# A gated three-branch decoder layer: two gates computed ahead of the stick-breaking branch, which is gated as it leaves PSUM, and the weight sums issued at other rates

## The chip, the core and the metric

The kernel runs on one core of a Trainium2 chip. Its engines are TensorE (PE, matrix products, whose results go to banks of the PSUM memory), VectorE (DVE) and ScalarE (ACT), which work on tiles of 128 partitions in SBUF or PSUM, GpSimd (POOL) and SyncE (SP), which here mostly issue DMA transfers. The metric is device time in microseconds, as the median of several runs; a single profiled execution gives the trace from which durations are read.

## The reference

One layer (batch 1, 512 tokens, model width 1024) with three causal token mixers: A differential attention (4 heads), B stick-breaking attention (8 heads), C dilated windows (4 heads in each of 3 groups). Each branch is projected to the model width, gated, and the three are summed:

```python
proj = x @ w_in          # q, k, v of the three mixers, and three gates of 1024 columns
o_da = diff_attention(...); o_sb = stick_breaking_attention(...); o_dl = dilated_attention(...)
g = jax.nn.sigmoid(gates).reshape(B, S, N_BRANCHES, D)
merged = (g[:, :, 0] * (o_da @ w_branch_da) + g[:, :, 1] * (o_sb @ w_branch_sb)
          + g[:, :, 2] * (o_dl @ w_branch_dil))
m = merged @ w_out
x = layer_norm(alpha * x + m, ln1_g, ln1_b)
c = jnp.square(jax.nn.relu(x @ w_up)) @ w_down
ple = jax.nn.sigmoid(x @ w_ple_gate) * (p @ w_ple)
x = layer_norm(alpha * x + c + ple, ln2_g, ln2_b)
```

Everything is float32.

## The kernel before

**Products.** A float32 product is made of three matmuls in a rounded format: each operand is split into a high part (a cast on ACT, L264) and the rest (a subtraction on DVE, L266), and high x high, high x low and low x high are summed in PSUM. Weights come in chunks of 128 x 1024 (512 KB): SP loads a chunk into one of 6 raw buffers (`fill`, L196), the two splits write one of 5 pairs of tiles (`split_next`, L240), and the matmuls read those. All other tiles of 128 x 512 come from one pool of 52 slots (`slot`, L76): a tile gets a slot when the last reader of the one before is done, be it an engine or a DMA.

**Seven products for eight.** Many of the large products are cut in 2 x 2 x 2 blocks and made with seven block products in place of eight (`seven`, L720, for gates; `value_pair`, L545; `group_items`, L355; and others). Four of the seven need sums of weight blocks. Most sums are made ahead in DRAM by DMAs that POOL issues, some of which add while they write (`sum_steps`, L1197): 15 targets or pairs of targets for the mixers, then those of the MLP, four at a time in turn. Others (products 7 and 3 of the value pair and the gates) are made by a DMA that adds onto a raw chunk once that chunk has been split (`then_add`, L173).

**The list of items.** The program is a list of items. An item is a burst of matmuls into a PSUM bank and an eviction, which is emitted after the next item's weights have been split. In order, with the item's number: the q, k and v projections of B (0 to 10), q and k of the dilated heads 0 and 1 and the values of group 0 (11 to 26), the values of A (27 to 30), the values of groups 1 and 2 as a "value pair" (31 to 44, 12 matmuls each), q and k of the dilated heads 2 and 3 in three groups of 7 items (45 to 58 and 63 to 69, 24 matmuls of 256 columns in each item), q and k of A (59 to 62 and 70 to 73). Then the branch of B (`first_branch`, L816, 8 items of 12 matmuls, 74 to 81), the gate of B (`gate_alone`, L758, 14 items of 12, 82 to 95), the gate and branch of C (`gate_chain`, L787, and `branch_seven`, L876, 14 items of 12 and 14 of 6, 96 to 123), the gate and branch of A (124 to 151), the output projection, the first LayerNorm, the gated embedding and the MLP.

**Gates.** `gate_alone` frees each PSUM bank at once: its evictions are copies and additions into SBUF. `gate_chain` keeps up to six banks over several products and evicts less. Both leave raw gates in `gate_raw`. `gate_sig` (L685) makes one sigmoid on ACT, and only after the last exponential of the heads. The branch of B leaves PSUM as a copy on ACT (L832) into a new slot; its gating is a multiplication on DVE in SBUF (`first_gate`, L943), spread over the eight items after `gated_at`.

**Heads.** The attention heads are generators beside the items: `step` (L2122) advances each active head by one part, once or twice per item, and starts new heads as PSUM banks allow. A dilated head (`dil_head`, L1962) makes its scores and weights, waits for the values, takes some further empty steps (L2057), transposes the weights and makes its second product (L2087 and L2092) with `values`, which `keep` (L533) stored to DRAM and `values_of` (L537) loads again in strided order. Both are DMAs that POOL issues. All heads must be done at `gated_at - 1`; what is left of them is emitted there at once. The outputs of the heads of B and C are stored to DRAM (`put_away`) and loaded again by SP (`bring_back`) 9 items ahead of their branch for B, 14 for C.

**Pacing.** After each item the loop adds size x rate to a credit and issues one step of the weight sums for each whole unit (L2203 to L2209). A sum's DMA also waits for a split (or an eviction) four marks back, so that sums are spread over the main stream. From `forms_at` (item 25) up to `gated_at`, weight splits are ordered behind the latest ACT and DVE work of the heads (`tied`, L2189).

Of the kernel before, what the change touches and what calls it, by code (L numbers as in the profile page):

```python
# [57 lines left out]
def trunk(tc, a, out):  # L58
    nc = tc.nc
    es = ExitStack()  # L60
    with es:
# [14 lines left out]
        def slot(name, dt=F32):  # L76
            return big.tile([P, 512], dt, name=nm(name), tag="s", bufs=NSLOT)
# [146 lines left out]
        tied = [False]  # L224
# [61 lines left out]
        items = []  # L286
# [68 lines left out]
        def group_items(gi, pairs):  # L355
# [21 lines left out]
            def add(ps, need, free, run, ev, bank):  # L377
                for p in ps:
                    at = {5: 0, 6: 1, 7: 2, 3: 3}.get(p)
                    cs[p] = [chunk(w[{1: 0, 2: 1, 4: 3}[p]] if at is None else qsum[gi][at], 1024)]  # L380
                item([c for p in free for c in cs[p]], lambda b: run(), lambda b: ev(),
                     need=[c for p in need for c in cs[p]], bank=bank)
                items[-1]["rate"] = 0.85

            def put(*args):
                with tc.high_priority():
# [158 lines left out]
        def value_pair(nv):  # L545


            pair_at.append(len(items))
            cs, s, x = {}, {}, {}
            w = [[a["wv"][nv + n, 2 * h + kp].rearrange("p k n -> p (k n)") for n in range(2) for h in range(2)]  # L550
                 for kp in range(2)]

            for p in (1, 2, 7, 6, 4, 5, 3):
                for r in range(2):
                    if not r:
                        cs[p] = [chained(cs, p, kp, w[kp], vsum[kp]) for kp in range(2)]

                    def bank(p=p, r=r):
                        if p == 5:
                            x[r] = at_bank()  # L560
                        return x[r] if p in (5, 3) else at_bank() if r else mm_bank()

                    def mm(ps, p=p, r=r):
                        for k in range(4):
                            c = cs[p][k // 2]
                            n = slice(k % 2 * 512, k % 2 * 512 + 512)
                            q = slice(r * P, r * P + P)
                            h, lo = [t[:, q] for t in xf[p][k]]
                            go, end = k == 0 and p != 3, k == 3 and p != 5
                            nc.tensor.matmul(ps, h, c["h"][:, n], start=go, stop=False, skip_group_check=True)  # L570
                            nc.tensor.matmul(ps, h, c["l"][:, n], start=False, stop=False, skip_group_check=True)
                            nc.tensor.matmul(ps, lo, c["h"][:, n], start=False, stop=end, skip_group_check=True)

                    def ev(ps, p=p, r=r):
                        if p in (1, 7):
                            s[p, r] = slot("dl_v")
                            nc.scalar.copy(s[p, r], ps)
                        elif p == 2:
                            t = slot("dl_v")
                            nc.vector.tensor_add(t, s[1, r], ps)  # L580
                            keep(1, r, t)
                        elif p == 6:
                            nc.vector.tensor_add(s[1, r], s[1, r], ps)
                            nc.vector.tensor_add(s[7, r], s[7, r], s[1, r])
                        elif p == 3:
                            nc.vector.tensor_add(s[1, r], s[1, r], ps)
                            keep(1, 2 + r, s[1, r])
                        else:
                            t = slot("dl_v") if p == 4 else s[7, r]
                            nc.vector.scalar_tensor_tensor(t, s[7, r], -1.0, ps, op0=OP.mult, op1=OP.subtract)  # L590
                            keep(2, r + 2 * (p == 5), t)
                    item(cs[p] if r else [], mm, ev, need=cs[p], bank=bank, size=0.5)
                    items[-1]["rate"] = 1.0

        def v_items(nv, name, g):
            cs = [chunk(a["wv"][nv, c].rearrange("p k n -> p (k n)"), 1024) for c in range(4)]
# [29 lines left out]
            for tt in range(4):  # L626
                def mm(ps, tt=tt):
                    if name != "sb_v" or tt > 1:
                        products(ps, tt, range(4))
                        yield  # L630
                        products(ps, tt, range(4, 8))
                        return
                    if not tt:
                        two[0], two[1] = ps, mm_bank()
                    products(two[0], 0, range(4 * tt, 4 * tt + 4))
                    if tt:
                        put(two[0], 0)
                    yield
                    products(two[1], 1, range(4 * tt, 4 * tt + 4))

                def ev(ps, tt=tt):
                    if name != "sb_v" or tt:
                        put(two[1] if name == "sb_v" and tt == 1 else ps, tt)
                first = name == "sb_v" and tt < 2
                item(cs if tt == 3 else [], mm, ev, need=cs[2 * tt:2 * tt + 2] if first else cs,
                     bank=((lambda: two[0]) if tt else at_bank) if first else None)
                items[-1]["rate"] = 1.0 if name == "da_v" else 2.4

        nt, nv = 2, 0
        pair_at = []  # L650
# [29 lines left out]
        merged = {}  # L680
# [4 lines left out]
        def gate_sig(i, tt, half):  # L685
            t, sign = gate_raw.pop((i, tt, half))

            with tc.issue_after(last_exp[0]):
                nc.scalar.activation(t, t, AF.Sigmoid, scale=sign)
            return t  # L690
# [125 lines left out]
        def first_branch():  # L816
            for half in range(2):
                cs = [chunk(a["wb"][half, c].rearrange("p k n -> p (k n)"), 1024) for c in range(2)]
                for tt in range(4):
                    def mm(ps, tt=tt, cs=cs):  # L820
                        q = slice(tt * P, tt * P + P)
                        for k in range(4):
                            c = cs[k // 2]
                            n = slice(k % 2 * 512, k % 2 * 512 + 512)
                            h, lo = oTs[4 + k]
                            nc.tensor.matmul(ps, h[:, q], c["h"][:, n], start=k == 0, stop=False)
                            nc.tensor.matmul(ps, h[:, q], c["l"][:, n], start=False, stop=False)
                            nc.tensor.matmul(ps, lo[:, q], c["h"][:, n], start=False, stop=k == 3)

                    def ev(ps, tt=tt, half=half):  # L830
                        t = slot("b1")
                        e = nc.scalar.copy(t, ps)  # L832
                        marks.append(getattr(e, "ins", e))
                        merged[tt, half] = t
                    item(cs if tt == 3 else [], mm, ev, need=cs, size=0.5,
                         bank=at_bank if tt == 1 and not half else None)
                    items[-1]["rate"] = 2.4

        bsum = {i: [dram.tile([P, 1024], F32, name=f"bsum{i}_{j}") for j in range(4)] for i in (0, 2)}
        of = {}  # L840
# [97 lines left out]
            item([], mm, ev, size=0.08)  # L938

        for j, it in enumerate(items):  # L940
            it.setdefault("rate", 3.0 if j < 12 else 2.8 if j < 24 else 0.0 if j < 27 else 2.1)

        def first_gate(tt, half):  # L943
            g = gate_sig(1, tt, half)
            nc.vector.tensor_mul(merged[tt, half], merged[tt, half], g)

        branch_at = {1: len(items)}
        first_branch()
        gate_alone(0, 1)
        gated_at = len(items)  # L950
        for n, i in ((1, 2), (2, 0)):
            gate_chain(n, i)
            if n == 1:
                for j, th in enumerate([(tt, half) for half in range(2) for tt in range(4)]):
                    items[gated_at + 2 + j]["pre"] = lambda th=th: first_gate(*th)
            branch_at[i] = len(items)
            branch_seven(i, {} if i else {(6, 0): [(0, 0, 0)], (6, 1): [(0, 0, 1)], (5, 1): [(1, 0, 0)],
                                          (3, 0): [(1, 0, 1)]})
# [1003 lines left out]
        def dil_head(hd):  # L1962
# [91 lines left out]
            if hd == 0:  # L2054
                yield
                values = values_of(hd)
            for _ in range({0: 4, 1: 1, 3: 1}.get(hd, 0)):  # L2057
                yield

            src0 = {}  # L2060
# [4 lines left out]
            for half in range(2):  # L2065
# [4 lines left out]
                t = slot("pt0")  # L2070
# [4 lines left out]
            for g in range(2):  # L2075
# [4 lines left out]
                t = slot("pt12")  # L2080
# [4 lines left out]
            for kb in range(4):  # L2085
                n = 256 if kb < 3 else P
# [71 lines left out]
        for n, it in enumerate(items):  # L2158
# [27 lines left out]
            pump(freed, {1: 3, 3: 0, 4: 0, ple_at: 0, ple_at + 1: 0}.get(n, 1 if n < 10 else 2))  # L2186
            if n == 8:
                tie.clear()
            tied[0] = forms_at <= n < gated_at  # L2189
            if n == gated_at:  # L2190
                tie.clear()
            if n == 4:
# [165 lines left out]
```

## Time and profile before

| | |
|---|---|
| median of 3 runs | 1044.06 us (1042.19, 1044.06 and 1699.26) |
| profiled execution | 1043.86 us, its span 1042.2 us |
| mean granted clock of TensorE | 0.994 |
| VectorE, ScalarE, GpSimd busy | 778.8, 613.1, 203.7 us |
| moved by DMA | 270.74 MB, mean 260 GB/s |
| first branch and gate of B in the trace | matmuls at L826 to L828 from 418.8 us, at L735 to L737 from 453.3 us |

The span runs from the first to the last instruction of the trace; the time of the execution is 1.7 us longer. In the profile, a row names line, engine, operation and the tiles written and read (out<-in); `wh` and `wl` are the high and low part of a weight chunk, `graw` a raw gate, `b` a branch, `dl_vh` the reloaded values, `at` and `mm` PSUM banks. Matmuls are pipelined, so the duration of one is longer than the distance to the next. The granted clock is 1 where TensorE runs at full speed.

### The profile page before, as it was taken

How to read it: one execution, taken by the hardware profiler on the slowest of the kernel's cores; microseconds unless marked ns; L12 is line 12 of the kernel's file. 1: busy time of each engine (PE TensorE's matmuls, PEld its weight loads, DVE VectorE, ACT ScalarE, POOL GpSimd, SP SyncE). 2: the span in 40 equal slices, each digit the busy share in tenths (PEclk: the TensorE clock that was granted, in tenths of full speed). 3: DMA queues.
4: the chain of work that ended last, by engine and by line, in shares of the span. 5: the costliest groups of instructions: out<-in, count | busy, mean ns of one | idle time of the engine just before them, and what ended most of it. 6: DMA issues, size and time to landing. Idle time of an engine off the chain costs nothing.

```text
span 1042.2 us, 15650 instructions
## 1 busy us (share of the span) xinstructions
PE 1024.0 (98%) x5650; PEld 885.6 (85%) x5650; DVE 778.8 (75%) x1387; ACT 613.1 (59%) x1057; POOL 203.7 (20%) x307
## 2 busy tenths in 40 slices
PE   9999999999989999999999999999999999999997
PEld 7888888887979898878888888889999899899886
DVE  6888566758646877668879795898778777777975
ACT  7565556655534566555775753676666556566651
POOL 0323331112243012211112131211111121101001
PEclk9999999999989999999999999999999999999999
DMA  8999998659999789688999996489999999988522
GB/s 307 295 276 293 247 300 269 172 141 271 319 324 319 248 261 283 144 222 204 288 289 256 291 344 210 107 215 362 318 304 339 311 323 345 295 270 286 179 83 81
DMA packets 79534, 270.74 MB, mean 260 GB/s; under 512 B 9721, under 2 KB 12553, under 8 KB 79457
## 3 DMA queue, kind: packets, MB, share of 16 engines
q0 software_dynamic: 36624, 130.89, 50.1%
q1 hardware_dynamic: 42256, 137.95, 36.1%
q8 instruction: 44, 0.72, 0.3%
q10 hardware_dynamic: 576, 0.92, 0.2%
q14 instruction: 34, 0.27, 0.1%
HBM read 262.35 MB, written 112.22 MB: 359 GB/s over the span
## 4 chain that ended last, share of the span: by engine, by line
PE 74%; DMA 10%; DVE 6%; issue 6%; ACT 2%; POOL 1%; DVEq 0%; POOLq 0%; ACTq 0%
PE mm L89 6%; PE mm L90 6%; PE mm L91 6%; PE at L1415 4%; PE at L1416 4%; PE at L1417 4%; PE at L735 3%; PE at L736 3%; PE at L737 3%; DMA qsum<-qsum 2%; DMA msum<-in_wgm_dram 2%; DMA values<-dl_v 2%; DVE wl L266 2%; PE at L91 1%; PE at L90 1%
## 5 line engine op out<-in xcount | busy, mean ns | idle before, releaser
L266 DVE TENSOR_TENSOR wl<-raw,wh 128x1024 fp32r<-128x1024 f32 x268 | 322.1, 1214 | 118.3 <-ACT wh L264 115.4
L264 ACT CAST wh<-raw 128x1024 fp32r<-128x1024 f32 x268 | 276.2, 1042 | 197.5 <-PE mm L90 94.7
L89 PE MATMUL mm<-xhT,wh 128*128 128x512 f32 (+1 forms) x254 | 95.7, 377 | 0.0
L91 PE MATMUL mm<-xhT,wl 128*128 128x512 f32 (+1 forms) x254 | 94.3, 371 | 0.0
L90 PE MATMUL mm<-xlT,wh 128*128 128x512 f32 (+1 forms) x254 | 94.1, 371 | 0.0
L1415 PE MATMUL at<-wh,hh 128*128 128x512 f32 x188 | 73.7, 392 | 0.0
L1416 PE MATMUL at<-wl,hh 128*128 128x512 f32 x188 | 73.7, 392 | 0.0
L89 PE MATMUL mm<-x1hT,wh 128*128 128x256 f32 x256 | 72.8, 284 | 0.7 <-ACT up L1343 0.7
L1417 PE MATMUL at<-wh,hl 128*128 128x512 f32 x188 | 73.1, 389 | 0.0
L90 PE MATMUL mm<-x1lT,wh 128*128 128x256 f32 x256 | 72.4, 283 | 0.0
L91 PE MATMUL mm<-x1hT,wl 128*128 128x256 f32 x256 | 72.4, 283 | 0.0
L91 PEld LDWEIGHTS mm<-xhT,wl 128*128 128x128 f32 x254 | 47.8, 188 | 8.3
L89 PEld LDWEIGHTS mm<-xhT,wh 128*128 128x128 f32 x254 | 47.9, 188 | 7.8 <-PE mm L604 0.2
L90 PEld LDWEIGHTS mm<-xlT,wh 128*128 128x128 f32 x254 | 48.0, 189 | 7.5
L89 PEld LDWEIGHTS mm<-x1hT,wh 128*128 128x128 f32 x256 | 48.9, 191 | 2.7 <-ACT up L1343 0.9
L90 PEld LDWEIGHTS mm<-x1lT,wh 128*128 128x128 f32 x256 | 48.9, 191 | 1.5
L91 PEld LDWEIGHTS mm<-x1hT,wl 128*128 128x128 f32 x256 | 48.9, 191 | 0.0
L1232 POOL DMA_DIRECT2D usum<-in_wu_dram x32 | 28.5, 899 | 99.6 <-DVE wl L266 38.4
L1232 POOL DMA_DIRECT2D dsum<-in_wd_dram x28 | 23.4, 835 | 116.5 <-DVE wl L266 48.3
L1417 PEld LDWEIGHTS at<-wh,hl 128*128 128x128 f32 x188 | 35.3, 188 | 7.7
L1415 PEld LDWEIGHTS at<-wh,hh 128*128 128x128 f32 x188 | 35.5, 189 | 6.1
L1416 PEld LDWEIGHTS at<-wl,hh 128*128 128x128 f32 x188 | 35.5, 189 | 5.7
(672 smaller groups left out, 2856.5 us busy)
## 6 DMA issues: line engine op xcount, KB each, us to landing
usum<-in_wu_dram POOLq DMA_DIRECT2D x48, 512.0 KB, 9.9
dsum<-in_wd_dram POOLq DMA_DIRECT2D x42, 512.0 KB, 8.6
raw<-usum SPq DMA_DIRECT2D x32, 512.0 KB, 8.2
raw<-dsum SPq DMA_DIRECT2D x28, 512.0 KB, 8.5
raw<-in_wt_dram SPq DMA_DIRECT2D x26, 512.0 KB, 7.3
raw<-in_wd_dram SPq DMA_DIRECT2D x25, 512.0 KB, 7.6
raw<-in_wu_dram SPq DMA_DIRECT2D x24, 512.0 KB, 8.0
raw<-in_wv_dram SPq DMA_DIRECT2D x18, 512.0 KB, 7.5
```

The costliest lines, as they stand in the source:

```text
L89: nc.tensor.matmul(ps, wh, xh, start=start, stop=False, skip_group_check=True)
L90: nc.tensor.matmul(ps, wh, xl, start=False, stop=False, skip_group_check=True)
L91: nc.tensor.matmul(ps, wl, xh, start=False, stop=stop, skip_group_check=True)
L264: i = nc.scalar.copy(h, raw)
L266: i = nc.vector.tensor_sub(lo, raw, h.bitcast(F32))
L735: nc.tensor.matmul(ps, h[:, q], c["h"][:, n], start=go, stop=False, skip_group_check=True)
L736: nc.tensor.matmul(ps, h[:, q], c["l"][:, n], start=False, stop=False, skip_group_check=True)
L737: nc.tensor.matmul(ps, lo[:, q], c["h"][:, n], start=False, stop=end, skip_group_check=True)
L1232: i = nc.gpsimd.dma_start(o, i, accum_op=OP.add, max_dma_last_dim=4096)
L1415: nc.tensor.matmul(ps, h[:, q], c["h"][:, s], start=go, stop=False, skip_group_check=True)
L1416: nc.tensor.matmul(ps, h[:, q], c["l"][:, s], start=False, stop=False, skip_group_check=True)
L1417: nc.tensor.matmul(ps, lo[:, q], c["h"][:, s], start=False, stop=end, skip_group_check=True)
```

## The change

Gate 1 (of B) and gate 2 (of C) are both made with `gate_alone`, ahead of `first_branch`, which moves from items 74 to 81 to items 102 to 109; `gated_at` moves from 96 to 102. The sigmoid of gate 1 is made ahead of each item of the first branch, and the branch is multiplied by it as it leaves PSUM, on DVE, into the gate's own tile. `first_gate` and the ACT copies go. Gate 0 (of A) stays a `gate_chain`. From item 110 on the list is the same.

The rate of the weight sums becomes 0.5 in the groups (from 0.85) and in the value pair (from 1.0), 2.4 in the values of A (from 1.0), and 2.1 in items 24 to 26 (from 0). Dilated head 0 takes six empty steps ahead of its second product (from four), head 1 two (from one). The splits are tied to the heads' work from item 43 up to the new `gated_at`.

```diff
@@ group_items, add
-                items[-1]["rate"] = 0.85
+                items[-1]["rate"] = 0.5
@@ value_pair
-                    items[-1]["rate"] = 1.0
+                    items[-1]["rate"] = 0.5
@@ v_items
-                items[-1]["rate"] = 1.0 if name == "da_v" else 2.4
+                items[-1]["rate"] = 2.4
@@ first_branch
                     def ev(ps, tt=tt, half=half):
-                        t = slot("b1")
-                        e = nc.scalar.copy(t, ps)
+                        t = merged[tt, half]
+                        e = nc.vector.tensor_mul(t, t, ps)
                         marks.append(getattr(e, "ins", e))
-                        merged[tt, half] = t
+
+                    def pre(tt=tt, half=half):
+                        merged[tt, half] = gate_sig(1, tt, half)
...
+                    items[-1]["pre"] = pre
@@ order of the items
-            it.setdefault("rate", 3.0 if j < 12 else 2.8 if j < 24 else 0.0 if j < 27 else 2.1)
-
-        def first_gate(tt, half):
-            g = gate_sig(1, tt, half)
-            nc.vector.tensor_mul(merged[tt, half], merged[tt, half], g)
-
+            it.setdefault("rate", 3.0 if j < 12 else 2.8 if j < 24 else 2.1)
+
+        gate_alone(0, 1)
+        gate_alone(1, 2)
         branch_at = {1: len(items)}
+        gated_at = len(items)
         first_branch()
-        gate_alone(0, 1)
-        gated_at = len(items)
         for n, i in ((1, 2), (2, 0)):
-            gate_chain(n, i)
-            if n == 1:
-                for j, th in enumerate([(tt, half) for half in range(2) for tt in range(4)]):
-                    items[gated_at + 2 + j]["pre"] = lambda th=th: first_gate(*th)
+            if not i:
+                gate_chain(n, i)
             branch_at[i] = len(items)
@@ dil_head
-            for _ in range({0: 4, 1: 1, 3: 1}.get(hd, 0)):
+            for _ in range({0: 6, 1: 2, 3: 1}.get(hd, 0)):
                 yield
@@ main loop
-            tied[0] = forms_at <= n < gated_at
+            tied[0] = pair_at[0] + 12 <= n < gated_at
```

## The prediction, on record before the changed kernel was run

> **What bounds the kernel now.** I read the page first, then the waits of TensorE, then the busy time by stage, then the chain of waits, and last the queues of POOL and DVE around the two waits that stand out.
>
> ```profile
> PE 1024.0 (98%) x5650; PEld 885.6 (85%) x5650; DVE 778.8 (75%) x1387; ACT 613.1 (59%) x1057; POOL 203.7 (20%) x307
> ...
> PEclk9999999999989999999999999999999999999999
> ```
>
> The first row is the busy time of each engine, the second the granted clock in 40 slices of the span. TensorE is busy 1024.0 of 1042.2 us, and its clock dips once in mid-kernel, in the twelfth slice (287 to 313 us). All a reordering can win lies in the missing 18.2 us and in matmuls that ran at a lower clock; the 5650 matmuls stay what they are.
>
> ```profile
> PE at L2087 <- DMA dl_vh<-values: 4.9, 1, 4.9
> PE mm L826 <- ACT b L832: 1.5, 1, 1.5
> ...
> PE at L571 <- DVE wl L266: 0.9, 1, 0.9
> ```
>
> These are the waits of TensorE: who waited, for whom, us in total, times, longest. The first is the second product of the dilated heads (L2087), which waits until its values have come back from DRAM. The second is the first branch (L826), which waits for a PSUM bank that ScalarE has still to copy out. The third is the value pair, short of a split weight.
>
> ```profile
> 280.00:300.00 20.00, 14.67 (x118) 13.99 (x117) 14.66 (x34) 10.18 (x19) 7.63 (x12) 0.92 1.00 317
> 300.00:320.00 20.00, 20.00 (x146) 19.06 (x145) 3.87 (x5) 5.63 (x10) 5.81 (x9) 0.91 1.04 328
> ...
> 440.00:460.00 20.00, 18.54 (x96) 15.33 (x94) 11.28 (x40) 11.61 (x27) 2.70 (x4) 1.00 0.83 214
> ```
>
> Each row is a stretch: busy us and count of instructions on PE, PEld, DVE, ACT and POOL, then the granted clock, the DMA share and GB/s. The long wait lies in 280 to 320, and the clock falls to 0.92 and 0.91 there; the shorter one in 440 to 460 leaves it at 1.00.
>
> ```profile
> 267.28 16.52 DMA values<-dl_v
> ...
> 291.23 7.89 DMA dl_vh<-values
> 299.25 4.75 PE at L2087 x12
> ...
> 434.18 1.52 PE at L2087 x8
> ...
> 439.34 9.70 DMA oT<-oT
> 449.14 0.59 ACT b L832
> ```
>
> This is the chain that ended last (start, us, what). The last stores of the values take 16.52 us to land; only then does POOL issue the last reloads, which land at 299.12, when L2087 can start. Its first 12 matmuls then take 4.75 us (396 ns each), against 1.52 us for 8 (190 ns each) later: that is the lower clock. The second wait is one of memory: the copy L832 needs a fresh slot, and gets the one that the store of a dilated output (oT) was still reading until 449.04.
>
> ```profile
> 272.80 0.56 POOL L534 DMA_DIRECT2D values<-dl_v  x1 [0.65 <-DMA dl_vh<-values]
> 282.92 0.84 POOL L1232 DMA_DIRECT2D bsum<-in_wbq_dram  x1 [9.56 <-DMA bsum<-bsum]
> 289.14 1.54 POOL L542 DMA_DIRECT2D dl_vh<-values  x2 [5.38 <-DMA values<-dl_v]
> ```
>
> These are POOL's issues around the first reloads (start, us, what, and in brackets the wait ahead and what ended it). Between the last store of values and the reloads POOL stood 9.56 us at a weight sum whose target had not landed, and then 5.38 us until the stores had.
>
> **The change part by part.** *Heads later.* Dilated head 0 gets two more steps ahead of its second product and head 1 one more. In the groups a step is an item of 24 matmuls, about 3.4 us (24 x 20.00/141, by the row of 260 to 280 below, where TensorE ran 141). So head 0 asks 6.8 us later and head 1 3.4 us later, and the wait was 4.9: for head 0 it is covered, for head 1 up to 1.5 us can stay if its reloads are the late ones. The work in between is the group's own matmuls, moved forward, not added. I take 0.5 us left: gain 4.4, ends 3.4 and 4.9. With it goes the low clock: 4.75 less 12 x 0.19 is 2.5 us; ends 0 (a wait of some us stays and the clock falls again) and 2.5.
>
> The Trainium skill, page "TensorE: Matmul & The Clock Gate", section "Part 1: The HAM clock gate", says that the clock halves after an idle window of about 3.4 us and returns after about 3.4 us of work. The trace agrees in the first half (4.9 us of idling lowered the clock, 1.5 did not). By that rule the slow spell costs at most half of 3.4, an estimate of 1.7 us in place of 2.5, and the sum below would end at 1037.1.
>
> *Sums.* Each item adds its size x rate to a credit, and each whole unit issues one step of a sum. The seven items ahead of the pair give 3 x 2.1 + 4 x 2.4 = 16 steps, where it was 3 x 0 + 4 x 1.0 = 4; the pair's 14 items 14 x 0.25, 4 with the carry, for 14 x 0.5 = 7; the next six group items 3 for 5 (0.5 and 0.85 each). From the branches on it is one step ahead (119 for 118). In all 12 transfers move forward, and 5 leave the stretch in which values are stored and reloaded.
>
> ```profile
> q0 software_dynamic: 36624, 130.89, 50.1%
> 160.00:180.00 20.00, 20.00 (x99) 16.65 (x98) 14.46 (x23) 13.81 (x21) 4.05 (x7) 1.00 0.81 272
> 180.00:200.00 20.00, 20.00 (x97) 16.61 (x96) 12.67 (x20) 13.19 (x21) 2.31 (x3) 1.00 0.71 222
> 200.00:220.00 20.00, 20.00 (x94) 16.63 (x93) 15.97 (x28) 10.88 (x20) 1.39 (x2) 1.00 0.43 79
> ...
> 260.00:280.00 20.00, 20.00 (x141) 18.75 (x140) 13.75 (x40) 9.02 (x22) 5.90 (x10) 1.00 1.03 311
> ```
>
> The first row is POOL's DMA queue: 50.1% of 1042.2 us for 130.89 MB, so 2.09 us of all engines for a 512 KB sum. Twelve take 25 us, and the three stretches from 160 to 220 have 0.19 + 0.29 + 0.57 of 20 us free, 21.0 us. So the DMA fills up there, with some 4 us spilling into the pair. TensorE was never idle in 260 to 280, where the share was 1.03, so a full DMA alone costs nothing there; POOL's queue does, if the additions behind it come late:
>
> ```profile
> 223.95 8.42 DMA raw<-in_wv_dram
> 232.45 1.06 ACT wh L264
> 233.53 0.98 DVE wl L266
> ```
>
> This is the one transfer of the pair that has no lead: the addition that makes the weights of its third product, issued by POOL, then cast and split by 234.51. The product starts at 235.16 and reaches that half of the weights six matmuls later, at about 236.5 (0.225 us each): 2.0 us of room. Ends: a gain of 0.9 (the wait at L571 goes with the thinner sums) and a loss of 2.1 (the 4.1 us spilled, less the room). The nearer is the first, since thinner sums in the pair also clear POOL's queue around it; the two partly cancel, and I take 0.
>
> *Two gates first, the branch gated out of PSUM.* The second gate as a "gate_alone" has the same 14 x 12 matmuls; its evictions become 12 on DVE and 4 on ACT, where the chain had 6 and 8. The branch loses 8 ACT copies, and the 8 multiplications that followed them become its eviction.
>
> ```profile
> L266 DVE TENSOR_TENSOR wl<-raw,wh 128x1024 fp32r<-128x1024 f32 x268 | 322.1, 1214 | 118.3 <-ACT wh L264 115.4
> ...
> L945 DVE TENSOR_TENSOR b<-b,graw 128x512 f32<-128x512 f32 x8 | 5.1, 686 | 0.0
> ...
> L832 ACT COPY b<-mm 128x512 f32<-128x512 f32 x7 | 4.0, 587 | 7.4 <-DMA oT<-oT 6.0 <-PE mm L828 1.3
> ...
> L802 DVE TENSOR_TENSOR graw<-graw,at 128x512 f32<-128x512 f32 x2 | 1.4, 680 | 0.0
> ```
>
> Columns: count, busy us, mean ns, idle before. DVE gains 6 x 0.680 = 4.1 us, ACT loses 12 copies of about 0.587, 7.0 us. Both are off the path while their stages have air. The fresh slots of the copies go, and with them the 1.5 us at L826 (ends 1.5 and 0: the oT reloads and two gates' results now share the slots with the last heads, where a branch's did). What is late next in the branch is DVE:
>
> ```profile
> 499.00:563.00 64.00, 64.00 (x284) 52.47 (x283) 53.78 (x73) 44.05 (x62) 10.30 (x14) 1.00 0.98 278
> ```
>
> This stretch holds the old gate chain, the multiplications and the second branch: 284 matmuls, 0.225 us each, 53.78 us of DVE. In the new order the first and second branch stand alone together, 8 x 12 + 14 x 6 = 180 matmuls, 40.6 us. DVE's work there is the same less the chain's 14 splits and 6 additions (17.0 + 4.1), plus the first branch's 4 weight splits and 4 splits of oT (4.9, and 2.4 at half the width): 40.0 us. It just fits, and part is done ahead in the second gate. Each multiplication must come within the next item (2.7 us, two banks) and can stand behind one split of 1.214. Ends: 0, and, if each of the 11 splits brings the mean idling of the row of L266 (118.3/268 = 0.44 us), 40.0 + 4.8 - 40.6 = 4.2 us. I take 0.8, near the lower end since that old stretch had DVE at 84% and no idle TensorE.
>
> *Moved with it.* The branch's four oT reloads on SP come 28 items later and right ahead of the next four; POOL's four additions of the second gate come 8 items earlier, their sums having been issued long before (by item 22 in both). The heads have 28 items to end in, not 22, and start later by two or three: nothing is flushed. The splits are tied to the heads' steps from pair item 12 on instead of six items ahead of the pair; no row shows that stretch untied; its ends are 0.9 either way, the wait at L571 that arose while it was tied, and I take 0.
>
> *Sum.* The profiled execution took 1043.9 (span 1042.2, the rest around it; the runs' median is 1044.1). 1043.9 - 4.4 - 2.5 - 1.5 + 0 + 0.8 = **1036.3 us**, 0.7% less.
>
> **The rivals.** *The reload stays late.* For it: 16.52 us of landing and the DMA at 1.03 around it, of which five sums of 2.09 us fewer take only 10 us away over the pair and the first group's items; dilated head 1 gets one step. Against: POOL's 9.56 us wait. If 2 to 4 us stay, the low clock with it at times, the time is 1036.3 - 0.5 + 3 + up to 2.5, about 1040.5.
>
> *DVE becomes the bound in the branches.* For it: 40.0 of 40.6 us. Against: 84% and no wait before. 1036.3 - 0.8 + 4.2 = 1039.7.
>
> *The sums that were moved forward block the pair: slower than before.* Place: the addition of 223.95. Price: were it to land in 16.52 us, as the stores did, in place of 8.42, then 8.1 - 2.0 = 6.1 us of idling, and 2.5 for the clock: 1036.3 + 8.6 = 1044.9. It decides from a landing of 15.5 us on (8.42 + 2.0 + 7.6 - 2.5). Against: in the pair's own items the sums are thinner. The Trainium skill, page "DMA: Bandwidth & Descriptors", section "Queues, rings and completion order", says that an engine takes the queues in turn and each queue in order. By that rule the addition stands behind all sums POOL issued before it, and the 4.1 us that spill are what delays it, an estimate of 2.1 us beyond the room and of 1038.4 us in all. No row of this case shows the order within a queue.
>
> **How the numbers follow.** The forecast gets 0.60 (1033 to 1039), the late reload 0.16, DVE 0.10, the blocked pair 0.10, more than I see 0.04. The lowest time the rows allow is 1043.9 less 4.9, 2.5, 1.5 and 0.9, 1034.1; mixing of heads and gates that the rows don't price may add 2 either way. Range 1031.5 to 1045.5. A measurement of this kernel can tell about 2% from no change; 2% is 21 us, and no case reaches it: faster 0.01, same 0.96, slower 0.03.
>
> **What would show it.** Right: no wait of TensorE at L2087 above 1.5 us, the clock at 1.00 in 280 to 320; no wait of the first branch for a slot; busy PE near 1021.5 us (1024.0 less 2.5, since matmuls at a low clock count as busy), span near 1034.6. The pair's third product within 1 us of the second. Wrong: a new wait at L570 to L572, or of the branch for DVE, or a reload landing after 302.

## The result, and the profile after

The changed kernel takes 1051.75 us (median of 4 runs, 1050.9 to 1053.35) where the kernel before takes 1044.39 on the same chip: a ratio of 1.0079, 95% interval 1.0057 to 1.0102. That is within 2%, but slower, 15 us above the forecast and outside its range. One run of the kernel before took 1699.26 us; it counts in that median, but not in the ratio. The profiled execution took 1051.24 us, its span 1049.5.

The busy time and the granted clock in 40 slices, from the page of the changed kernel:

```profile
PE 1023.4 (98%) x5650; PEld 885.7 (84%) x5650; DVE 782.5 (75%) x1393; ACT 606.4 (58%) x1045; POOL 204.4 (19%) x307
...
PE   9999999679999999999999999999999999999997
...
PEclk9999999879999999999999999999999999999998
```

TensorE's busy time hardly moved (1024.0 before). The dip of the clock has moved from the twelfth slice to the eighth and ninth, where TensorE now also stands idle. The waits of TensorE in the changed kernel name what it waits for there:

```profile
PE mm L602 <- DVE dl_k L347: 12.7, 1, 12.7
PE at L1861 <- DVE al L1850: 1.8, 1, 1.8
...
PE at L735 <- DVE graw L808: 1.1, 1, 1.1
```

The two waits of before on which the forecast stood are not in this list: none at L2085 (the reload, L2087 before) and none of the first branch. In their place stands a wait of 12.7 us in the values of A (L602), for an eviction of a dilated key (L347) on DVE. The busy time by stage, same columns as before:

```profile
180.00:200.00 20.00, 20.00 (x97) 16.62 (x96) 9.28 (x12) 13.09 (x21) 7.25 (x11) 1.00 1.03 276
200.00:220.00 20.00, 5.55 (x19) 4.07 (x18) 7.26 (x14) 1.40 (x3) 0.00 (x0) 0.61 0.70 179
...
280.00:300.00 20.00, 19.87 (x153) 19.08 (x152) 11.76 (x42) 9.75 (x26) 2.85 (x4) 1.00 0.93 295
300.00:320.00 20.00, 20.00 (x164) 19.73 (x163) 15.03 (x31) 10.97 (x17) 9.06 (x14) 1.00 0.92 291
...
440.00:460.00 20.00, 20.00 (x106) 17.06 (x105) 15.46 (x43) 10.88 (x23) 3.08 (x5) 1.00 0.77 215
```

The stretches 280 to 320 and 440 to 460 are whole again, at full clock (the first branch itself now runs from 524 to 546 us, see below). The loss lies in 200 to 220: 19 matmuls where there were 94, at a clock of 0.61, and the DMA share ahead of it, in 180 to 200, has gone from 0.71 to 1.03. DVE's queue there (start, us, what, wait ahead and what ended it):

```profile
197.19 0.42 DVE L1819 TENSOR_TENSOR sm<-e 128x256 f32<-128x256 f32 x1
212.74 0.69 DVE L704 TENSOR_TENSOR xr<-xr,xr 128x512 f32<-128x512 f32 x1 [15.14 <-DMA xr<-in_xT_dram]
213.35 0.29 DVE L1821 CAST smp<-sm 128x256 fp32r<-128x256 f32 x1
213.56 0.68 DVE L347 COPY dl_k<-mm 128x512 f32<-128x512 f32 x1
```

L704 is the first subtraction of the value pair's operand forms (`mixer_forms`). It needs blocks of x that SP loads afresh from DRAM (`load_xr`, L519: eight blocks of 256 KB). In DVE's order the eviction at L347 stands behind it. DVE started nothing from 197.6 to 212.74, though the product that L347 copies out was complete at 194.6 (its last matmul, at L91, started at 194.16 and took 0.40); the PSUM bank stayed full, and TensorE waited. In the kernel before the eviction came first, and the subtraction had no wait:

```profile
196.07 0.69 DVE L347 COPY dl_k<-mm 128x512 f32<-128x512 f32 x1
...
198.61 1.29 DVE L704 TENSOR_TENSOR xr<-xr,xr 128x512 f32<-128x512 f32 x2
```

The x blocks by their tile (count, duration of an issue in ns, first and last start, and landing times in us), before and after:

```profile
L519 SPq DMA_DIRECT2D xr<-in_xT_dram x8: 385/419/710, 184.3 to 187.9; - x8
...
DMA to landing us min/median/max: 4.1/5.6/6.3
```

```profile
L519 SPq DMA_DIRECT2D xr<-in_xT_dram x8: 392/672/3059, 183.8 to 194.9; - x8
...
DMA to landing us min/median/max: 11.6/20.3/24.9
```

The first is issued at the same time as before (183.8; 184.3 before), and the median block lands 15 us later. Their eight issues also took SP 11.46 us in place of 4.33. In the chain that ended last, the block for which DVE waited was issued at 191.71 and took 20.94 us:

```profile
191.71 20.94 DMA xr<-in_xT_dram
```

What lies ahead of the blocks and beside them is POOL's sums: five steps in the kernel before, and 14 in the changed kernel, of which the first and the last are shown:

```profile
168.76 0.54 POOL L1234 DMA_DIRECT2D bsum<-in_wbq_dram  x1
169.29 1.04 POOL L1234 DMA_DIRECT2D msum<-in_wgm_dram  x2
177.33 0.52 POOL L1234 DMA_DIRECT2D bsum<-in_wbq_dram  x1 [7.00 <-DVE wl L266]
...
189.53 0.85 POOL L1232 DMA_DIRECT2D msum<-in_wgm_dram  x1 [7.01 <-DVE wl L266]
```

```profile
167.19 0.53 POOL L1232 DMA_DIRECT2D bsum<-in_wbq_dram  x1 [4.19 <-DVE wl L266]
...
196.71 0.81 POOL L1230 DMA_DIRECT2D msum<-in_wgm_dram  x1 [1.55 <-DMA msum<-msum]
```

### The profile page after: what moved, and what is told of

The parts are those of the page before. It is cut to its first block, busy times and chain, and to the rows that moved or that the text cites. A ratio compares the mean times of both kernels' runs of the same rounds, so it can differ in the third digit from the quotient of the medians.

```text
span 1049.5 us, 15631 instructions
## 1 busy us (share of the span) xinstructions
PE 1023.4 (98%) x5650; PEld 885.7 (84%) x5650; DVE 782.5 (75%) x1393; ACT 606.4 (58%) x1045; POOL 204.4 (19%) x307
## 3 DMA queue, kind: packets, MB, share of 16 engines
q0 software_dynamic: 36624, 130.89, 49.3%
q1 hardware_dynamic: 42256, 137.95, 35.7%
## 4 chain that ended last, share of the span: by engine, by line
PE 92%; DVE 4%; DMA 2%; ACT 1%; issue 1%; DVEq 0%
PE mm L89 9%; PE mm L90 9%; PE mm L91 9%; PE at L1413 4%; PE at L1414 4%; PE at L1415 4%; DMA xr<-in_xT_dram 2%; PE at L735 2%; PE at L737 2%; PE at L736 2%; PE mm L604 2%; PE mm L603 2%; PE at L91 2%; PE at L90 2%; PE at L89 2%; PE mm L602 2%
## 5 line engine op out<-in xcount | busy, mean ns | idle before, releaser
L91 PE MATMUL mm<-xhT,wl 128*128 128x512 f32 (+1 forms) x254 | 94.3, 371 | 0.0
L91 PE MATMUL mm<-x1hT,wl 128*128 128x256 f32 x256 | 72.4, 283 | 0.0
L91 PEld LDWEIGHTS mm<-xhT,wl 128*128 128x128 f32 x254 | 47.8, 188 | 8.3
L1230 POOL DMA_DIRECT2D usum<-in_wu_dram x32 | 28.9, 903 | 107.3 <-DVE wl L266 52.1
L91 PEld LDWEIGHTS mm<-x1hT,wl 128*128 128x128 f32 x256 | 48.9, 191 | 0.0
L602 PE MATMUL mm<-wh,xhT 128*128 128x512 f32 x88 | 35.3, 401 | 12.7 <-DVE dl_k L347 12.7
```

The costliest lines, as they stand in the source:

```text
L91: nc.tensor.matmul(ps, wl, xh, start=False, stop=stop, skip_group_check=True)
L602: nc.tensor.matmul(ps, x1, c["h"][:, s], start=k == 0, stop=False)
L1230: i = nc.gpsimd.dma_start(o, i, accum_op=OP.add, max_dma_last_dim=4096)
```

## The experiments

Three theories stood at first. A: the sums that moved ahead fill the DMA, the x blocks land late, and DVE's queue stands behind them. B: the splits, tied later, changed DVE's order and made the wait. C: the two gates, or the eviction on DVE, cost the time. None of the kernels leaves out any part of the computation. In e1, e5 and e10 the MLP's credit is 0.66 in place of 0.63, so that the last sums are issued in time; e6 and e9, without it, have the same time, so it is not what their gain comes from. In the last column, "none" means no wait of TensorE above 0.3 us.

| run | against | median us | ratio to before, 95% | x blocks land (median) | longest wait in 195 to 222 |
|---|---|---|---|---|---|
| e1 sums not ahead | after | 1031.96 | 0.9897 (0.9872 to 0.9922) | 5.6 | none |
| e2 sums ahead alone | before | 1053.48 | 1.0106 (1.0073 to 1.0138) | 20.5 | 13.3 |
| e3 tied as before | after | 1052.23 | 1.0099 (1.0069 to 1.0129) | 20.4 | 13.7 |
| e4 x loaded earlier | after | 1035.52 | 0.9935 (0.9914 to 0.9956) | 10.1 | none |
| e5 steps as before | e1 | 1032.30 | 0.9904 (0.9876 to 0.9931) | 5.7 | none |
| e6 sums thick in the pair | e1 | 1031.64 | 0.9897 (0.9870 to 0.9924) | 5.4 | none |
| e7 reorder alone | before | 1041.68 | 0.9987 (0.9972 to 1.0001) | 5.6 | none |
| e8 half the sums ahead | after | 1034.08 | 0.9919 (0.9892 to 0.9946) | 8.1 | 1.4 |
| e9 reorder and untied | e7 | 1032.51 | 0.9907 (0.9892 to 0.9921) | 6.4 | none |
| e10 tied, sums not ahead | e1 | 1032.91 | 0.9913 (0.9897 to 0.9930) | 5.7 | none |
| e11 subtract later | after | 1036.16 | 0.9941 (0.9917 to 0.9964) | 27.7 | none |
| e12 other half ahead | after | 1044.67 | 1.0022 (1.0011 to 1.0033) | 16.2 | 7.3 |

**e1, the sums back to their old place in items 24 to 30**

```diff
-            it.setdefault("rate", 3.0 if j < 12 else 2.8 if j < 24 else 2.1)
+            it.setdefault("rate", 3.0 if j < 12 else 2.8 if j < 24 else 0.0 if j < 27 else 2.1)
...
-                items[-1]["rate"] = 2.4
+                items[-1]["rate"] = 1.0 if name == "da_v" else 2.4
...
-                credit += 0.63
+                credit += 0.66
```

> The changed kernel with the sums of items 24 to 30 at their old rates (0 and 1.0), the rest of the change kept (and the MLP's credit 0.66 in place of 0.63, so that the last sums are in time). Theory A (the twelve sums issued ahead of the pair fill the DMA, the x blocks land 15 us late, and DVE's queue stands behind their first subtraction): the wait of TensorE at L602 of 12.7 us goes, the x blocks land in 5 to 8 us, time 1051.8 - 17 = about 1035 us. Theory B (the untied splits let the subtraction ahead of the eviction in DVE's order, whatever the DMA does): a wait at L602 stays, time above 1045. Theory C (the two gates and the branch's eviction on DVE are what costs): time stays near 1051.

All of the loss goes, and the kernel is 1.0% faster than before. After the start of the kernel (a wait of 1.2 us that every run has) no wait of TensorE above 0.7 us is left.

**e2, the sums ahead and nothing else, in the kernel before** (the first two lines of that diff, the other way round)

> The kernel before with only the rates of items 24 to 30 raised (2.1 and 2.4). Theory A: the x blocks land in 15 to 25 us, DVE waits for them at L704, TensorE waits 8 us or more for an eviction behind it, the wait at L2087 stays, time 1044.4 + 10 to 17 = 1054 to 1061 us. Theory B: with the splits still tied, DVE's order puts the evictions first and TensorE waits under 4 us there, time under 1049. Theory C: no change, 1044.

The loss is there without the rest of the change; 1053.48 us is just under the 1054 to 1061 expected. DVE's row at the subtraction and the longest wait of TensorE in e2:

```profile
212.80 1.35 DVE L704 TENSOR_TENSOR xr<-xr,xr 128x512 f32<-128x512 f32 x2 [14.94 <-DMA xr<-in_xT_dram]
```

```profile
PE at L1863 <- DVE al L1852: 13.3, 1, 13.3
```

Here the splits are tied as before, and another instruction (al) is the one that TensorE waits for; the stall is the same. So neither the untied splits (B) nor the two gates (C) made it. One thing expected did not come: the wait for the reload is not in e2's list. L2087 waits 1.9 us for DVE (`pt`) instead, behind a stall that had already held everything up.

**e3, the ties of before in the changed kernel**

```diff
-            tied[0] = pair_at[0] + 12 <= n < gated_at
+            tied[0] = forms_at <= n < gated_at
```

> The changed kernel with the splits tied from item 25 on, as before. Theory A: the x blocks still land late and TensorE still waits 10 us or more, time 1048 to 1053 us. Theory B: the wait falls under 4 us, time about 1037 to 1042.

No better, with a wait of 13.7 us at L1861. The ties do set DVE's order, as B said: with them (before, e2, e3) the eviction of dl_k runs ahead of the subtraction, without them (the changed kernel, e1, e8, e12) behind it. But the stall comes with either order, since `al` stands behind the subtraction too: B falls as the cause.

**e4, the x blocks loaded three items earlier, all sums ahead**

```diff
-        forms_at = pair_at[0] - 6
+        forms_at = pair_at[0] - 9
...
-            for _ in range(6):
+            for _ in range(12):
```

> The changed kernel with all its rates, but the loads of the x blocks issued three items earlier, ahead of the sums, and six more empty steps before they are used. Theory A: the x blocks land before the sums fill the DMA or at least long before they are subtracted, the wait at L602 goes, time about 1035 us (up to 1040 if the pair's own added weights are late behind the sums). Theory B: the order in DVE's queue is as in the changed kernel, a wait stays, above 1045. Theory C: 1051.

The wait goes, though the DMA stays full through the stretch. The windows of e4:

```profile
160.00:180.00 20.00, 20.00 (x99) 16.66 (x98) 14.14 (x22) 13.12 (x20) 4.54 (x8) 1.00 1.02 353
180.00:200.00 20.00, 20.00 (x96) 16.60 (x95) 13.15 (x21) 13.78 (x22) 8.07 (x11) 1.00 1.04 291
200.00:220.00 20.00, 20.00 (x94) 16.64 (x94) 16.85 (x29) 11.81 (x20) 4.48 (x6) 1.00 0.93 177
```

TensorE never stops. The 3.6 us by which e4 is slower than e1 have one visible cause: a wait of 2.5 us in the last gate (L735 for the eviction L808, until 582.2 us), and behind it half clock from 583.4 to 586.9 us, some 1.8 us more. The changed kernel has that wait with 1.1 and e1 has not. What brings it was not tried; e8 and e12, with half of the sums ahead, do not have it.

**e8 and e12, half of the sums ahead each.** e8 puts items 24 to 26 back at rate 0, e12 the values of A back at 1.0.

> The changed kernel with the rate of items 24 to 26 back at 0; the values of A keep 2.4, so that some 5.6 of the 12 sums move ahead. It leaves nothing out. Theory A in proportion (each sum of 2.09 us in the queues ahead of the x blocks delays them): they land after a median of 11 to 14 us, DVE stands 5 to 9 us at L704, TensorE waits 3 to 6 us, 1035 to 1040. Rival (only a full queue hurts: the smaller burst finds 0.2 to 0.3 of the DMA free and is hidden): landing under 9 us, no wait above 1 us, 1031 to 1033.

> The changed kernel with the rate in the values of A back at 1.0; items 24 to 26 keep 2.1, so that some 6.3 of the 12 sums move ahead, those that are issued before the x blocks. It leaves nothing out. Theory I (the delay grows faster than the number of sums, with little cost while the DMA still has room: e8 with 5.6 sums gave a landing of 8.1 us and 1034.1): landing 7 to 11 us, DVE stands up to 4 us, 1032 to 1036. Theory J (only sums issued ahead of the blocks delay them, those issued beside them don't): landing 14 us or more, a wait of TensorE of 5 us or more, 1038 to 1046.

POOL's rows of these kernels give the count of sum steps issued from 167 us up to the first x load (near 184) and, behind the stroke, from there to the last sum of the burst: before 4 / 1, e8 6 / 2, e12 8 / 4, the changed kernel 8 / 6. The blocks land after 5.6, 8.1, 16.2 and 20.3 us. Two more sums ahead (and one beside) cost 2.5 us of landing, four (and three) cost 10.6; so the delay grows faster than the number. Theory J, that the sums beside the blocks cost nothing, does not hold: two more beside them alone, from e12 to the changed kernel, add 4.1. From e8 to e12 both counts rise by two and the landing by 8.1, so how much of that is due to those ahead is not separated. DVE's stand in e8 and in e12:

```profile
199.51 0.69 DVE L704 TENSOR_TENSOR xr<-xr,xr 128x512 f32<-128x512 f32 x1 [1.58 <-DMA xr<-in_xT_dram]
```

```profile
207.67 0.69 DVE L704 TENSOR_TENSOR xr<-xr,xr 128x512 f32<-128x512 f32 x1 [9.74 <-DMA xr<-in_xT_dram]
```

1.58 us of standing cost TensorE 1.4, 9.74 cost 7.3 + 1.8: beyond the free lead nearly every microsecond is passed on. For e8 I had expected 3 to 6 us of waiting in proportion, and its rival none; it lies between. For e12 the landing, the wait and the time are those of J, and theory I's 1032 to 1036 us was far too low: its thought, growth faster than the number, holds, but four more sums ahead and three beside were already past the cheap part.

**e11, the blocks as late as before, but used later**

```diff
-            for _ in range(6):
+            for _ in range(12):
```

> The changed kernel, all 12 sums ahead and the x blocks loaded at the same place, but twelve empty steps in place of six between their loads and their use, which puts the first subtraction (L704) behind the evictions dl_k and da_v in the order of DVE. It leaves nothing out. Theory A, second half (the late blocks cost only because DVE's queue is in order and evictions stand behind the subtraction): blocks still land after a median of 15 to 21 us, but no wait of TensorE at L602 or L1861 above 2 us, 1033 to 1037. Rival (the full DMA or late weights cost the time by themselves, and the subtraction is a bystander): TensorE still waits 8 us or more between 200 and 220, 1042 to 1052.

The windows and the longest wait of e11:

```profile
180.00:200.00 20.00, 20.00 (x96) 16.61 (x96) 11.60 (x18) 13.09 (x21) 8.00 (x11) 1.00 1.05 277
200.00:220.00 20.00, 20.00 (x94) 16.65 (x94) 9.92 (x16) 8.29 (x13) 4.49 (x6) 1.00 1.05 251
```

```profile
PE at L2019 <- DVE r L2011: 1.6, 1, 1.6
```

The blocks land even later (27.7 us), the DMA is full for 40 us, and TensorE does not stop in that stretch. This settles the second half of A: the stall between 200 and 220 comes from what stands behind the blocks' reader in DVE's queue, not from the late blocks or the full DMA by themselves. Of the 4.2 us by which e11 is slower than e1, the wait at L2019 is 1.6; the rest I did not follow.

**e5 and e6: which part took the reload's wait away?** D: the later steps of the heads; E: the thinner sums. e5 is e1 with the steps of before, e6 is e1 with the rates of before in the pair and the groups.

```diff
-            for _ in range({0: 6, 1: 2, 3: 1}.get(hd, 0)):
+            for _ in range({0: 4, 1: 1, 3: 1}.get(hd, 0)):
```

> The kernel of e1 (sums of items 24 to 30 as before, all else changed; 1032.0 us) with the empty steps of dilated heads 0 and 1 back at four and one. It leaves nothing out. Theory D (the later heads cover the reload): the wait at L2087 comes back with 2 to 5 us, with a lower clock in 280 to 320, and the time is 1035 to 1039. Theory E (the thinner sums in the pair and groups cover it, since POOL's queue and the DMA are clear when the values are stored and reloaded): no wait above 1 us, 1031 to 1033.

> The kernel of e1 with the rates of the weight sums in the value pair and the groups back at 1.0 and 0.85; the later steps of the heads stay. It leaves nothing out. Theory D: the six and two steps are enough, no wait at L2087 above 1 us, 1031 to 1033. Theory E: a wait of 2 to 5 us at L2087, a lower clock behind it, 1035 to 1039. Both can hold in part: then e5 and e6 both show a wait of 1 to 3 us.

Neither brings the wait back. So each is enough, or neither is needed and a third part does it.

**e7 and e9: the reorder alone, and the reorder with the new ties**

> The kernel before with the new order alone: both gates ahead of the first branch, the branch gated as it leaves PSUM; rates, steps and ties as before. It leaves nothing out. By the prediction: no wait of the first branch for a slot (1.5 us in the kernel before), the wait at L2087 as before (about 5 us and the low clock), 1041 to 1042. Theory C (two gates or the eviction on DVE cost time): a wait of TensorE for DVE at the first branch or the gates of 1 to 4 us, 1043 to 1047.

> The kernel of e7 (new order alone; a wait of 5.6 us at L2085, 1041.7 us) with one line more of the change: splits tied to the heads' work only from pair item 12 on. Steps, and all rates of sums, as before. It leaves nothing out. Theory F (the ties held the pair's splits, and so the stores of the values, back; later steps or thinner sums are not needed): no wait above 1.5 us at L2085, the last reload issued ahead of 288, 1031 to 1034. Theory G (steps or thin sums, either is enough and one is needed): the wait stays between 3 and 5.6 us with the low clock, 1037 to 1041.

e7 loses the wait of the first branch and keeps that of the reload; its median gain is 0.13%, 1.4 us (the interval goes from a gain of 2.9 to a loss of 0.1, so the time alone does not show it), with no new wait for DVE in the branches: C falls too. e9 differs from e7 by one line and gains 0.8% more. The rows of POOL that store the last values and issue the last reloads, in e7 and in e9:

```profile
274.04 0.56 POOL L534 DMA_DIRECT2D values<-dl_v  x1 [0.51 <-DVE ma L2001]
...
290.40 1.54 POOL L542 DMA_DIRECT2D dl_vh<-values  x2 [5.30 <-DMA values<-dl_v]
```

```profile
268.61 0.58 POOL L534 DMA_DIRECT2D values<-dl_v  x1 [0.49 <-DMA dl_vh<-values]
...
283.51 1.56 POOL L542 DMA_DIRECT2D dl_vh<-values  x2 [3.35 <-DMA values<-dl_v]
```

With the splits free of the heads' work DVE splits the pair's weights sooner (of the 18 splits that start between 205 and 272 us in both, the first at 217.0 in place of 221.7 us, the last at 266.3 in place of 269.1); the waits at L571 (0.9) and L2021 (0.8) of e7 are gone in e9, the values are stored 5.4 us sooner and the reloads are issued 6.9 us sooner, more than the 5.6 us for which TensorE waited in e7.

**e10, the ties of before in e1**

> The kernel of e1 (1032.0 us) with the splits tied as before, from forms_at on; later steps and thinner sums stay. It leaves nothing out. Theory F: the stores of the values come late again, a wait of 1 to 4 us at L2085 or L571 and 1034 to 1039. Theory G: the steps and the thinner sums cover it, no wait above 1 us, 1031 to 1033.

```profile
PE at L571 <- DVE wl L266: 0.9, 1, 0.9
```

```profile
283.25 2.29 POOL L542 DMA_DIRECT2D dl_vh<-values  x3 [13.30 <-DMA values<-dl_v]
```

The small wait at L571 returns, that of the reload does not: here the thinner sums leave POOL free, so that nothing but the stores' landing delays the reloads, and the steps are later too. So F and G each hold in part: the untied splits do it alone (e9), and the later steps with the thinner sums do it together (e10). Whether one of those two would do it alone was not tried, since e5 and e6 also have the untied splits. The gain of the reload was bought twice.

## Why the prediction was wrong, by its own steps

*The reload and the clock behind it (4.4 and 2.5).* Right: no wait at L2085, clock 1.00 in 280 to 320. (The second term is a little large: in the kernel before TensorE worked at half clock from 299.25 to 303.6 us, 4.35 us, which costs about 2.2.) The reason given, the later steps, is not shown: e5 and e9 do without them, and in e10 they stand together with the thinner sums.

*The slot of the first branch (1.5).* Right: the wait at L826 is gone from the changed kernel and from e7, and the new place of the first branch (below) is full. The median gain of e7, which has only this, is 1.4 us, in line with the term but not clear of noise.

*DVE in the branches (a loss of 0.8, up to 4.2 as a rival).* Too dear. In the changed kernel the first branch runs from 524 to 546 us, and DVE stood idle ahead of its eviction L832, waiting for TensorE, 6.9 us over four of its eight times. DVE was ahead, and TensorE was busy throughout:

```profile
520.00:546.00 26.00, 26.00 (x116) 21.38 (x115) 17.24 (x28) 9.18 (x13) 6.42 (x10) 1.00 1.03 292
```

*The ties (0).* Mis-sized: alone worth 0.8%, 8.3 us (e7 to e9), though in the whole change they gain nothing that the steps and thinner sums did not gain too, beyond the 0.9 us at L571 that e10 has and e1 has not.

*The sums (0): the step that failed.* It failed in two sentences. The first set 25 us of moved transfers against 21.0 us of room in 160 to 220. But POOL issues them as fast as its waits allow, 14 steps in 30 us, and the kernel before has its room elsewhere. Its windows while the x blocks are on their way, the last three columns being clock, DMA share and GB/s:

```profile
183.00:186.00 3.00, 3.00 (x15) 2.49 (x14) 1.59 (x3) 2.05 (x4) 0.00 (x0) 1.00 0.65 221
186.00:189.00 3.00, 3.00 (x15) 2.48 (x15) 1.59 (x2) 2.04 (x4) 0.00 (x0) 1.00 0.87 263
189.00:192.00 3.00, 3.00 (x19) 2.47 (x19) 0.93 (x2) 1.15 (x2) 0.85 (x1) 1.00 1.07 354
192.00:195.00 3.00, 3.00 (x16) 2.46 (x15) 0.89 (x2) 2.16 (x5) 0.00 (x0) 1.00 1.10 345
```

From 183 to 195 there are 0.35 + 0.13 of 3 us free, 1.4 us; most of the 21.0 us of room comes after the subtraction at 198.6, too late to help. Nine more steps at 2.09 us are 18.8 us. The second sentence called the addition at 223.95 "the one transfer of the pair that has no lead". The x blocks were not on the list at all. They are issued 14.4 us ahead of their use (184.26 to 198.61) and took up to 6.3 us to land; the eighth issue ended 4.3 us after the first began, so that some 4 us were to spare. In the changed kernel the block came 15.1 us after DVE stood ready for it. So the term put at 0 was a loss: e1, which takes back these early sums (and changes the MLP's credit), is 1.8% faster than the changed kernel. The rival that the sums would make it slower had the right cause, but the wrong place (L178 at 223.95, no wait there in the changed kernel) and too low a price, 1044.9.

*"A full DMA alone costs nothing there."* True for TensorE, as e4 and e11 show, but it was used for transfers whose lead nobody had looked up.

The account: the changed kernel against e1 is 1.0079 / 0.9897, 1.8%, 19 us. The waits at L602 and L1861 make 14.5; from 217.4 to 221.4 TensorE ran at half clock, a loss of 2; L735 took 1.1. Some 1.4 us are not traced. On the other side e1 gains 10.7 us on before: the 8.4 us that the forecast named, the 0.5 of the reload's wait that it had left standing, 0.9 at L571, and 0.9 that I did not follow.

## What to carry over

When background transfers are moved, list every load that is in flight in the stretch they move to, with its lead (issue to use, less its landing time) and what is queued behind its reader on the in-order engine; the load with the least lead sets the price, not the mean share of the DMA. Compare the burst with the room in the windows between issue and use, a few microseconds wide, not with the room of the whole stage. A change of several parts can hide its good parts under one bad one, and two good ones can buy the same wait: run each alone, since here the same kernel without its early sums is 1.0% faster than before, not 0.8% slower.

## What the runs showed of the hardware

A 256 KB load on SP's queue took 5.6 us to land (median of eight) with five sums of POOL issued around it and 20.3 us with fourteen, although it is on another queue, and issuing eight of them held SP for 11.46 us in place of 4.33: here the full DMA was felt at the issuing engine too.

TensorE's clock fell to one half after quite short waits: behind 1.9 us of waiting in e2 (L2087, half clock from 311.1 to 314.7 us) and 2.5 us in e4 (L735, from 583.4 to 586.9 us). Waits of 1.4 us in e8, 1.5 in the kernel before and 1.6 in e11 left it at 1.00.

The Trainium skill, page "DMA: Bandwidth & Descriptors", section "Queues, rings and completion order", says that each DMA engine takes the queues that have work in turn, a packet at a time. In the changed kernel SP's queue moved 137.95 MB in 35.7% of 1049.5 us, 2.7 us for a MB, and POOL's 130.89 MB in 49.3%, 1.45 times as long for a byte. By that rule the eight blocks, 2.1 MB or 5.7 us alone, beside one busy queue of POOL would take 5.7 x 2.45 = 14 us, an estimate. In the trace the block that DVE waited for was there 28.9 us after the first was issued (183.8 to 212.7), and in e12 23.6 us after. So the trace agrees that a load isn't spared by being on its own queue, but turns of that kind give half of this time. Of the 28.9 us, 7.9 had gone before SP issued that block (at 191.71); why issuing and landing both took so long stays open.
